# Low parts and one difference made by accumulating transfers in a decoder layer in fp32

## The chip, the cores and the metric

The kernel runs on one core of one Trainium2 chip. The metric is the device time of one launch in microseconds (us), the median of several runs. The names of the engines: PE is TensorE (matmuls), DVE is VectorE, ACT is ScalarE, POOL is GpSimd, SP is SyncE, which here only issues transfers.

## The reference

One decoder layer over 1024 tokens with model width 1024: a token mixer with two kinds of attention, then a feed-forward part (FFN) with a short convolution and a gate, width 2816, then a final norm. The change lies in the FFN and the final norm, and touches nothing of the attention.

```python
def rmsnorm(x, g):
    y = x32 * lax.rsqrt(jnp.mean(x32 * x32, axis=-1, keepdims=True) + EPS)
    return (y * g.astype(jnp.float32)).astype(x.dtype)

def conv_ffn(x, norm_g, w_up, conv_w, conv_b, w_down):
    S = x.shape[1]
    h = rmsnorm(x, norm_g) @ w_up
    hp = jnp.pad(h, ((0, 0), (CONV_W - 1, 0), (0, 0)))
    hc = conv_b
    for i in range(CONV_W):
        hc = hc + hp[:, i:i + S] * conv_w[i]
    gate, up = jnp.split(hc, 2, axis=-1)
    return (jax.nn.silu(gate) * up) @ w_down

def reference(x, attn_norm, ..., final_norm):
    h = h + token_mixer(rmsnorm(h, attn_norm[l]), ...)
    h = h + conv_ffn(h, ffn_norm[l], w_up[l], conv_w[l], conv_b[l], w_down[l])
    return rmsnorm(h, final_norm)
```

## The kernel before

**Arithmetic.** All products are to be good to fp32. A matrix is split into a high part, which is a copy rounded to the type fp32r, and a low part, which is the rest: low = x - high, rounded as well. A product is the sum of three passes (`acc3`, L1005 to L1008): high x high, high x low and low x high. ACT makes the high part with a copy, and `sub` makes the low part by a subtraction: on DVE its line is L95, on POOL L97. PE reads the low part of a weight block in the third matmul of the first three.

**Stages.** Attention takes the first 650 us, the product with w_o the next 72 (`wo_tiles`). During these the residual x is formed and its squares are summed for the FFN's norm: `cols` sums columns with ones on PE (L173), `rows` makes the reciprocal root on DVE and ACT (`rmv` L178, `rmt` L179, `rmr` L180 to L183) and spreads it over the partitions with PE (L193), and eight steps scale x by it (L1042 on DVE, high part `nh` L1047 on ACT, low part `nl` L95 on DVE).

**The FFN's up product** (722 to 1153 us) is made in 22 pairs, a gate block and an up block of 128 columns each. A pair is computed as seven products of half size, j = 0 to 6 (`Pair.run`), whose weights are a11, s2, a12, s3, s1, a22, s4: j = 0, 2 and 5 are plain halves of loaded blocks, the others are sums and differences of them. `Weights.parts` (L1138) makes the high and the low part of one of the seven. A product has 12 matmuls of 128x512. The parts are made six products ahead (AHEAD). In the first five pairs (CROWDED) all sums and all low parts are made on DVE, later ones are shared with POOL. For the first three pairs products 6 and 3 run early (`run_early`), into q, which ACT evacuates (L1172). DVE evacuates the others to hg and u (L1192), and the convolution and the gate run on ACT and DVE (L1080 to L1092).

**The FFN's down product** (from 1153 us) is made in seven products as well, in the order of the list `down`: "2", then "6" and "5" step by step in turn, then "1" and "7" in turn, "4" and "3", each of 11 steps k over 128 rows. `fetch_down` loads four steps ahead, `prep_down` makes the operands two steps ahead on DVE (L1277) and their parts on ACT (L1314) and DVE (L95). At "6" s2 = st - a11 is formed, of two k in one tile (`s`); "5" uses st; at "3" s2 becomes a12 - s2, for which a12 is loaded again (L1253). The results of products are summed into c and p tiles of two blocks of 128 columns each (L1335), and x is added by accumulating transfers issued by POOL (L1338): such a transfer reads memory and adds to what stands in the tile.

**The end.** The last three steps of "3" are held back and run in two halves of 256 tokens (`tail`, 128x256 matmuls). Each half is summed, squared, scaled by the final norm and its gains, and written out. Six of eight blocks of 128 columns are scaled by DVE straight from PSUM (L1419), two by POOL (L1460).

**Order.** Each engine runs its instructions in one fixed order, which a scheduler of the program sets when the kernel is built; `later(n, ...)` delays a step by n products. Each engine waits at an instruction until its inputs are there, and all behind it wait too. Transfers issued by SP and by POOL are queued on their engine the same way.

Of the kernel before, what the change touches and what calls it, by code (L numbers as in the profile page):

```python
# [17 lines left out]
P = 128  # L18
# [31 lines left out]
def body(ctx: ExitStack, tc: tile.TileContext, io, out):  # L50
# [1063 lines left out]
    class Weights:  # L1114
# [23 lines left out]
        def parts(self, j, new):  # L1138
            x = self.get(("a11", "s2", "a12", "s3", "s1", "a22", "s4")[j])
            t = new([P, 2, 4, P], F32R, "wp")  # L1140
            act(t[:, 0], x, AF.Copy)  # L1141
            sub("dve" if j % 2 or self.m < CROWDED else "pool", t[:, 1], x, t[:, 0])
            return t
# [101 lines left out]
    def fetch_down(i):  # L1245
# [5 lines left out]
        def get(n, ap):  # L1251
            live[n, k] = t = half([P, 512], name=n)
            load(t, ap)  # L1253

        if name in "23":
            get("a12", bottom[:, :512])
        if name in "24":
            get("b21", hid_d[KF + k][:, :512])
# [12 lines left out]
    def prep_down(i):  # L1271
# [15 lines left out]
        elif name == "6":  # L1287
            live["st", k] = st = big([P, 2, 512], name="st")
            if k % 2 == 0:
                t = big([P, 2, 512], name="s2")  # L1290
                live["s2", k], live["s2", k + 1] = t[:, 0], t[:, 1]
            a, b = live["s2", k], half([P, 512], name="t2")
            tt(dve, st[:, 0], a21, add, g["a22"])
            tt(dve, st[:, 1], b12, minus, b11)
            tt(dve, a, st[:, 0], minus, a11)
            tt(dve, b, g["b22"], minus, st[:, 1])
# [12 lines left out]
        else:  # L1309
            a, b = g["s2"], g["b22"]  # L1310
            tt(dve, a, g["a12"], minus, a)
        ops[name, k] = wide([P, 2, 512], F32R, "wp"), big([P, 2, 512], F32R, "bp")
# [55 lines left out]
    def after(name):  # L1368
# [4 lines left out]
        elif name in "65":  # L1373
            block_tiles("p" + name)
            for m in range(4):
                act(at("p" + name, m), b[m], AF.Copy)
        elif name == "1":
# [19 lines left out]
        elif name == "4":  # L1397
# [14 lines left out]
            for m in range(4):  # L1412
                later(12 + 2 * m, lambda m=m: outs[1].add(at("p5", m)))
            for m in (2, 3):
                later(20 + m, lambda m=m: act(at("p5", m), at("p5", m), AF.Copy, scale=col(C_ON + 4 + m)))

# [9 lines left out]
    def tail():  # L1426
# [9 lines left out]
        for t in range(2):  # L1436
            s = slice(t * 256, (t + 1) * 256)
            for m in (0, 2, 1, 3):
# [7 lines left out]
                if m < 3:  # L1446
                    sum_into(dve, outs[1].sq[:, s], q, outs[1].sq[:, s])
                sq[t] = q
                if t == 1 and m == 2:
                    cols(0)  # L1450
        rs[0] = rms_rows(None, rc[0])
        cols(1)
        for t in range(2):
# [4 lines left out]
            act(r, rs[t], AF.Copy)  # L1458
            y = res["p5"][1][:, :, s]
            pool.tensor_tensor(out=y, in0=y, in1=r[:, None, :].to_broadcast([P, 2, 256]), op=OP.mult)  # L1460
            for m in range(KD - 2):
                finish("c12" if m < 4 else "p5", m % 4, m, s, rs[t], 1)
            put_out(KD - 2, 1, s, y)

# [142 lines left out]
```

## Time and profile before

| | before |
|---|---|
| median of 3 runs | 1388.72 us (1386.17 to 1388.74) |
| profiled execution, its own time | 1389.71 us |
| its span in the profile | 1387.9 us |
| PE busy | 1348.8 us (97%) |
| DVE busy | 1022.8 us (74%) |
| ACT busy | 669.5 us (48%) |
| POOL busy | 412.0 us (30%) |

The span runs from the first to the last instruction of the profile. A matmul's row gives its start and its modelled length; since matmuls overlap, the distance between two starts says more than the length. In a row of the timeline what stands in brackets is the idle time ahead of the instruction and the instruction that ended it. PEclk is the granted clock of TensorE, 1.00 for its full speed of 2.4 GHz; its other level is 1.2 GHz.

### The profile page before, as it was taken

How to read it: one execution, taken by the hardware profiler on the slowest of the kernel's cores; microseconds unless marked ns; L12 is line 12 of the kernel's file. 1: busy time of each engine (PE TensorE's matmuls, PEld its weight loads, DVE VectorE, ACT ScalarE, POOL GpSimd, SP SyncE). 2: the span in 40 equal slices, each digit the busy share in tenths (PEclk: the TensorE clock that was granted, in tenths of full speed). 3: DMA queues.
4: the chain of work that ended last, by engine and by line, in shares of the span. 5: the costliest groups of instructions: out<-in, count | busy, mean ns of one | idle time of the engine just before them, and what ended most of it. 6: DMA issues, size and time to landing. Idle time of an engine off the chain costs nothing.

```text
span 1387.9 us, 18985 instructions
## 1 busy us (share of the span) xinstructions
PE 1348.8 (97%) x6996; PEld 1088.5 (78%) x6996; DVE 1022.8 (74%) x1626; ACT 669.5 (48%) x1213; POOL 412.0 (30%) x363
## 2 busy tenths in 40 slices
PE   9999999999999999999998999999999999999996
PEld 7788888767777767778887778888888888888785
DVE  5465465677766666684689997777878778998796
ACT  6032124667666555672445544444444444354362
POOL 4300524043334334210000035665666550000100
PEclk9999999999999999999999999999999999999998
DMA  5323436011121145744741222222221247743543
GB/s 212 130 96 101 157 107 199 15 46 40 50 72 49 43 125 146 210 140 147 257 145 42 80 91 92 77 75 76 91 91 71 73 146 258 277 165 138 153 140 122
DMA packets 69117, 164.58 MB, mean 119 GB/s; under 512 B 9288, under 2 KB 22744, under 8 KB 69024
## 3 DMA queue, kind: packets, MB, share of 16 engines
q1 hardware_dynamic: 56624, 132.16, 28.6%
q0 software_dynamic: 9520, 26.61, 6.4%
q10 hardware_dynamic: 2880, 4.60, 0.9%
q8 instruction: 55, 0.90, 0.3%
q14 instruction: 38, 0.31, 0.1%
HBM read 126.25 MB, written 37.09 MB: 118 GB/s over the span
## 4 chain that ended last, share of the span: by engine, by line
PE 59%; DVE 23%; ACT 7%; issue 4%; POOL 4%; DMA 1%; DVEq 0%; ACTq 0%; POOLq 0%
PE A L632 8%; PE O L669 8%; DVE wp L95 7%; PE B L654 6%; PE A L203 4%; PE A L204 4%; PE A L206 4%; PE B L1006 3%; PE B L1008 3%; PE B L1007 3%; PE A L1006 3%; PE A L1008 3%; ACT hc L1080 3%; PE A L1007 3%; DVE hg L1192 3%
## 5 line engine op out<-in xcount | busy, mean ns | idle before, releaser
L643 ACT ACTIVATE p<-p,low 128x640 f32<-128x640 f32 (+7 forms) x192 | 142.6, 744 | 48.7 <-DVE low L640 46.6
L1006 PE MATMUL B<-hi,wp 128*128 128x512 f32 x340 | 132.8, 391 | 1.0 <-DVE hg L1192 1.0
L1007 PE MATMUL B<-lo,wp 128*128 128x512 f32 x340 | 132.4, 390 | 0.0
L1008 PE MATMUL B<-hi,wp 128*128 128x512 f32 x340 | 132.2, 389 | 0.0
L654 PE MATMUL B<-ident,p 128*128 128x128 f32 x816 | 122.8, 275 | 4.4 <-ACT pt L609 1.6
L97 POOL TENSOR_TENSOR wp<-w,wp 128x512 fp32r<-128x512 f32 x34 | 56.3, 1657 | 229.3 <-ACT wp L1141 229.3
L654 PEld LDWEIGHTS B<-ident,p 128*128 128x128 f32 x816 | 96.2, 140 | 22.5 <-issue 5.8
L1141 ACT ACTIVATE wp<-ws 128x512 fp32r<-128x512 f32 x88 | 53.6, 628 | 99.9 <-DVE ws L1135 64.7
L95 DVE TENSOR_TENSOR wp<-ws,wp 128x512 fp32r<-128x512 f32 x54 | 66.9, 1243 | 44.6 <-ACT wp L1141 44.6
L203 PE MATMUL A<-hi,hi 128*128 128x512 f32 (+1 forms) x228 | 89.8, 394 | 1.5 <-DVE z L211 1.5
L609 ACT ACTIVATE pt<-B 128x512 f32<-128x512 f32 (+3 forms) x134 | 64.2, 480 | 52.0 <-PE B L654 51.4
L612 DVE COPY pt<-B 128x512 f32<-128x512 f32 (+3 forms) x154 | 77.4, 509 | 15.9 <-PE B L654 15.0
L204 PE MATMUL A<-lo,hi 128*128 128x512 f32 (+1 forms) x228 | 88.8, 390 | 0.0
L1080 ACT ACTIVATE hc<-hg,prm 128x1024 f32<-128x1024 f32 x44 | 54.5, 1243 | 66.3 <-DVE hg L1192 66.2
L103 ACT ACTIVATE hi<-w 128x1024 fp32r<-128x1024 f32 (+2 forms) x34 | 34.7, 1023 | 96.2 <-PE A L204 61.5
L1082 DVE SCALAR_TENSOR_TENSOR hc<-hg,prm,hc 128x1022 f32<-128x1022 f32 x44 | 78.1, 1775 | 0.6
L1006 PE MATMUL A<-nh,wp 128*128 128x512 f32 x188 | 74.3, 395 | 3.7 <-ACT q L1172 3.7
L669 PE MATMUL O<-pt,vsw 128*64 128x256 f32 x528 | 76.4, 387 | 0.0
L1081 DVE SCALAR_TENSOR_TENSOR hc<-hg,prm,hc 128x1023 f32<-128x1023 f32 x44 | 58.1, 1320 | 24.0 <-ACT hc L1080 23.9
L1006 PEld LDWEIGHTS B<-hi,wp 128*128 128x128 f32 x340 | 64.0, 188 | 14.9 <-issue 1.3
L1007 PEld LDWEIGHTS B<-lo,wp 128*128 128x128 f32 x340 | 64.0, 188 | 13.3 <-DVE lo L95 0.2
L1008 PEld LDWEIGHTS B<-hi,wp 128*128 128x128 f32 x340 | 63.9, 188 | 13.3
(328 smaller groups left out, 3667.1 us busy)
## 6 DMA issues: line engine op xcount, KB each, us to landing
w<-in_w_up SPq DMA_DIRECT2D x50, 512.0 KB, 3.3
hidd<-hid SPq DMA_DIRECT2D x22, 512.0 KB, 2.6
w<-in_w_down SPq DMA_DIRECT2D x22, 512.0 KB, 3.4
a<-in_w_down SPq DMA_DIRECT2D x44, 256.0 KB, 4.9
b<-hidd SPq DMA_DIRECT2D x33, 256.0 KB, 5.1
w<-in_w_o SPq DMA_DIRECT2D x16, 512.0 KB, 3.4
x<-in_xT SPq DMA_DIRECT2D x15, 512.0 KB, 6.3
rb<-scr POOLq DMA_DIRECT2D x48, 128.0 KB, 2.9
```

Source lines behind the costliest of these rows:

```text
L95: dve.tensor_tensor(out=o, in0=a, in1=f(b), op=OP.subtract)
L203: mm(outs[c], wh, hs[c], start=start, stop=False)
L204: mm(outs[c], wh, ls[c], start=False, stop=False)
L632: mm(a[:, s, :w], lh, rh[:, s * w:(s + 1) * w], start=j == 0, stop=j == len(passes) - 1)
L643: act(p, p, AF.Exp, bias=low, scale=-1.0, accum_out=r["total"])
L654: nc.tensor.transpose(b[:, k * P:(k + 1) * P], self.rows[y]["p"][:, (4 * q + k) * P:(4 * q + k + 1) * P], ident)
L669: mm(o[64 * x:64 * x + 64, z * P:2 * P], self.value(x, k), self.pt[x, k // 4][:, k % 4, z:, :], start=k == 0, stop=k == last - 1, skip_gro ...
L1006: mm(b, wh, h, start=start, stop=False, skip_group_check=skip)
L1007: mm(b, wh, l, start=False, stop=False, skip_group_check=skip)
L1008: mm(b, wl, h, start=False, stop=stop, skip_group_check=skip)
L1080: later(n, lambda: act(o, x, AF.Identity, bias=col(C_CB + m), scale=w[2]))
L1082: later(n + 6, lambda: dve.scalar_tensor_tensor(o[:, 2:], x[:, :T - 2], w[0], o[:, 2:], op0=OP.mult, op1=OP.add))
```

## The change

There are three parts.

- In the first five pairs, the low parts of j = 0, 2 and 5 (the plain weights) are no longer subtracted on DVE. ACT writes the negative of the high part into the low part's place (L1144 of the changed kernel), and a transfer issued by POOL (L1146) adds the weight block from memory to it, 256 KB each, 15 in all.
- The difference `s` of "6" is stored with the other sign, a11 - st. The product of "6" is evacuated with scale -1 for that. Transfers issued by POOL add a12 from memory (L1265, five of 512 KB and one of 256 KB), so that "3" finds a12 - s2 there. The 11 loads of a12 and the 11 subtractions at "3" are gone.
- At the end ACT multiplies c12 and p5 by the gains first (in 128x256 and 128x512 pieces, `gain`), and the last step is one multiplication per two blocks, 128x2x256: three on DVE and one on POOL for each half (L1476).

```diff
@@ -1139,7 +1139,13 @@
             x = self.get(("a11", "s2", "a12", "s3", "s1", "a22", "s4")[j])
             t = new([P, 2, 4, P], F32R, "wp")
             act(t[:, 0], x, AF.Copy)
-            sub("dve" if j % 2 or self.m < CROWDED else "pool", t[:, 1], x, t[:, 0])
+            if j in (0, 2, 5) and self.m < CROWDED:
+
+                act(t[:, 1], f(t)[:, 0], AF.Copy, scale=-1.0)
+                k = 4 if j else 0
+                side(t[:, 1], io["w_up"][self.m + (NF if j == 5 else 0)][:, k:k + 4], accum_op=OP.add)
+            else:
+                sub("dve" if j % 2 or self.m < CROWDED else "pool", t[:, 1], x, t[:, 0])
             return t
 
     def block_product(o, w, j, start, stop):
@@ -1252,8 +1258,12 @@
             live[n, k] = t = half([P, 512], name=n)
             load(t, ap)
 
-        if name in "23":
+        if name == "2":
             get("a12", bottom[:, :512])
+        if name == "4" and k % 2 == 0:
+            n = min(2, KF - k)
+            side(live["s2pair", k][:, :n], io["w_down"][(KF + k) * P:(KF + k + n) * P, :512]
+                 .rearrange("(k p) m -> p k m", k=n), accum_op=OP.add)
         if name in "24":
             get("b21", hid_d[KF + k][:, :512])
         if name in "64":
@@ -1287,12 +1297,12 @@
         elif name == "6":
             live["st", k] = st = big([P, 2, 512], name="st")
             if k % 2 == 0:
-                t = big([P, 2, 512], name="s2")
+                live["s2pair", k] = t = big([P, 2, 512], name="s2")
                 live["s2", k], live["s2", k + 1] = t[:, 0], t[:, 1]
             a, b = live["s2", k], half([P, 512], name="t2")
             tt(dve, st[:, 0], a21, add, g["a22"])
             tt(dve, st[:, 1], b12, minus, b11)
-            tt(dve, a, st[:, 0], minus, a11)
+            tt(dve, a, a11, minus, st[:, 0])
             tt(dve, b, g["b22"], minus, st[:, 1])
         elif name == "5":
             a, b = g["st"][:, 0], g["st"][:, 1]
@@ -1308,7 +1318,6 @@
             tt(dve, b, b, minus, b11)
         else:
             a, b = g["s2"], g["b22"]
-            tt(dve, a, g["a12"], minus, a)
         ops[name, k] = wide([P, 2, 512], F32R, "wp"), big([P, 2, 512], F32R, "bp")
         for x, t in ((a, ops[name, k][0]), (b, ops[name, k][1])):
             act(t[:, 0], x, AF.Copy)
@@ -1373,7 +1382,7 @@
         elif name in "65":
             block_tiles("p" + name)
             for m in range(4):
-                act(at("p" + name, m), b[m], AF.Copy)
+                act(at("p" + name, m), b[m], AF.Copy, scale=-1.0 if name == "6" else 1.0)
         elif name == "1":
             block_tiles("p1")
             for m in range(4):
@@ -1411,8 +1420,12 @@
             outs[1] = Out()
             for m in range(4):
                 later(12 + 2 * m, lambda m=m: outs[1].add(at("p5", m)))
-            for m in (2, 3):
-                later(20 + m, lambda m=m: act(at("p5", m), at("p5", m), AF.Copy, scale=col(C_ON + 4 + m)))
+            for m in range(4):
+                later(20 + m, lambda m=m: gain("p5", m, 4 + m, slice(0, 512)))
+
+    def gain(name, j, m, s):
+        x = at(name, j)[:, s]
+        act(x, x, AF.Copy, scale=col(C_ON + m))
 
     def finish(name, j, m, s, rs, c):
         x = at(name, j)[:, s]
@@ -1446,6 +1459,7 @@
                 if m < 3:
                     sum_into(dve, outs[1].sq[:, s], q, outs[1].sq[:, s])
                 sq[t] = q
+                gain("c12", m, m, s)
                 if t == 1 and m == 2:
                     cols(0)
         rs[0] = rms_rows(None, rc[0])
@@ -1456,11 +1470,11 @@
                 rs[1] = rms_rows(None, rc[1])
             r = half([P, 256], name="rst")
             act(r, rs[t], AF.Copy)
-            y = res["p5"][1][:, :, s]
-            pool.tensor_tensor(out=y, in0=y, in1=r[:, None, :].to_broadcast([P, 2, 256]), op=OP.mult)
-            for m in range(KD - 2):
-                finish("c12" if m < 4 else "p5", m % 4, m, s, rs[t], 1)
-            put_out(KD - 2, 1, s, y)
+            for e, by, name, j in ((pool, r, "p5", 1), (dve, rs[t], "c12", 0), (dve, rs[t], "c12", 1),
+                                   (dve, rs[t], "p5", 0)):
+                y = res[name][j][:, :, s]
+                e.tensor_tensor(out=y, in0=y, in1=by[:, None, :].to_broadcast([P, 2, 256]), op=OP.mult)
+                put_out(2 * j + (4 if name == "p5" else 0), 1, s, y)
 
     h1.fetch(0)
     wo_prep(0)
```

The instructions move in three places that matter for what follows. On DVE, ahead of the first norm of the FFN, the rows are these before (wp: weight parts; ws: sums of weights; rmv to rmr: the norm's row chain; rs: its spread copy):

```order
L1135 TENSOR_TENSOR ws_7091<-ws_7089,w_7082 128x512
L95 TENSOR_TENSOR wp_7099<-ws_7089,wp_7099 128x512
L95 TENSOR_TENSOR wp_7109<-w_7105,wp_7109 128x512
L95 TENSOR_TENSOR wp_7093<-ws_7091,wp_7093 128x512
L95 TENSOR_TENSOR wp_7102<-w_7083,wp_7102 128x512
L178 TENSOR_SCALAR rmv_7131<-B_7126 128x4
L180 RECIPROCAL rmr_7133<-rmt_7132 128x4
L181 SCALAR_TENSOR_TENSOR rmt_7132<-rmr_7133 128x4
L182 TENSOR_TENSOR rmt_7132<-rmt_7132,rmv_7131 128x4
L183 SCALAR_TENSOR_TENSOR rmr_7133<-rmt_7132,rmr_7133 128x4
L197 COPY rs_7152<-B_7153 128x512
```

and these after:

```order
L1135 TENSOR_TENSOR ws_7092<-ws_7090,w_7082 128x512
L95 TENSOR_TENSOR wp_7101<-ws_7090,wp_7101 128x512
L178 TENSOR_SCALAR rmv_7135<-B_7130 128x4
L95 TENSOR_TENSOR wp_7094<-ws_7092,wp_7094 128x512
L180 RECIPROCAL rmr_7137<-rmt_7136 128x4
L181 SCALAR_TENSOR_TENSOR rmt_7136<-rmr_7137 128x4
L182 TENSOR_TENSOR rmt_7136<-rmt_7136,rmv_7135 128x4
L183 SCALAR_TENSOR_TENSOR rmr_7137<-rmt_7136,rmr_7137 128x4
L197 COPY rs_7156<-B_7157 128x512
```

Two low parts that stood directly ahead of `rmv` are gone (two more a little further up are gone too), and one more low part now stands behind it.

On PE, at the turn from pair 3 to pair 4, the rows are these before (A and B: PSUM banks; nh, nl, hi, lo: parts of the tokens):

```order
L1006 MATMUL B_7696<-hi_7278,wp_7558 128x512
L1007 MATMUL B_7696<-lo_7279,wp_7558 128x512
L1008 MATMUL B_7696<-hi_7278,wp_7558 128x512
L1006 MATMUL A_7749<-nh_7166,wp_7627 128x512
L1007 MATMUL A_7749<-nl_7167,wp_7627 128x512
L1008 MATMUL A_7749<-nh_7166,wp_7627 128x512
L1006 MATMUL A_7749<-nh_7166,wp_7627 128x512
L1007 MATMUL A_7749<-nl_7167,wp_7627 128x512
```

and these after, from the last three of pair 3's a22 on:

```order
L1006 MATMUL B_7643<-hi_7317,wp_7593 128x512
L1007 MATMUL B_7643<-lo_7318,wp_7593 128x512
L1008 MATMUL B_7643<-hi_7317,wp_7593 128x512
L1006 MATMUL A_7764<-nh_7170,wp_7639 128x512
L1007 MATMUL A_7764<-nl_7171,wp_7639 128x512
L1008 MATMUL A_7764<-nh_7170,wp_7639 128x512
L1006 MATMUL B_7710<-nh_6810,wp_7614 128x512
L1007 MATMUL B_7710<-nl_6811,wp_7614 128x512
```

Before, pair 4's a11 (wp_7627) runs ahead of pair 3's a22 (wp_7582); after, pair 4's a11 (wp_7639) comes behind it (wp_7593), 12 matmuls later, and is left after three matmuls for other work.

On POOL, behind its last product of the gate, the rows of the changed kernel are these (s: the stored differences of "6"; c and p: results to which x is added):

```order
L1092 TENSOR_TENSOR hid_10289<-hc_10205,hc_10206 128x1024
L1092 TENSOR_TENSOR hid_10449<-hc_10337,hc_10338 128x1024
L1265 DMA s_10573<-in_w_down 128x2x512
L1265 DMA s_10663<-in_w_down 128x2x512
L1265 DMA s_10765<-in_w_down 128x2x512
L1265 DMA s_10865<-in_w_down 128x2x512
L1265 DMA s_10965<-in_w_down 128x2x512
L1265 DMA s_11058<-in_w_down 128x512
L1347 DMA c_11617<-x2d 128x2x512
L1347 DMA c_11618<-x2d 128x2x512
L1347 DMA p_11170<-x2d 128x2x512
```

Before, the transfers into c follow the rows of L1092 directly. The six new ones stand between them, and each waits only for the subtractions that fill its tile.

## Rows read from the trace of the kernel before

**Rows 1.** Waits of PE in 700 to 860 us: total, times, longest.

```profile
PE A L1006 <- ACT q L1172: 3.7, 1, 3.7
PE B L1006 <- DVE hg L1192: 3.6, 2, 2.6
```

**Rows 2.** Waits of PE in 1325 to 1388 us.

```profile
PE A L1006 <- ACT wp L1314: 1.9, 1, 1.9
```

**Rows 3.** Stretches: length, then busy us of each engine, PEclk, DMA share, GB/s.

```profile
800.00:820.00 20.00, 18.54 (x81) 14.74 (x79) 19.83 (x21) 9.65 (x14) 9.57 (x5) 1.00 0.28 97
820.00:840.00 20.00, 18.82 (x76) 15.43 (x77) 14.80 (x16) 7.97 (x11) 8.42 (x5) 0.91 0.23 88
```

**Rows 4.** Timeline of PE, 736 to 744 us: start, length, engine, line, operation.

```profile
737.83 0.79 PE L1006 MATMUL A<-nh,wp 128*128 128x512 f32 x1 [3.67 <-ACT q L1172]
...
743.54 0.41 PE L1007 MATMUL B<-lo,wp 128*128 128x512 f32 x1
```

**Rows 5.** Timeline of PE, 765 to 797 us.

```profile
765.65 0.39 PE L1008 MATMUL B<-hi,wp 128*128 128x512 f32 x1
...
796.58 0.39 PE L1007 MATMUL A<-nl,wp 128*128 128x512 f32 x1
796.81 0.39 PE L1008 MATMUL A<-nh,wp 128*128 128x512 f32 x1
```

**Rows 6.** Line L1277: duration min/median/max in ns, first and last start.

```profile
L1277 DVE TENSOR_TENSOR s<-a,s x11: 676/681/683, 1332.2 to 1362.4; 128x512 f32<-128x512 f32 x11
```

**Rows 7.** Chain that ended last, 715 to 830 us: start, length, what.

```profile
787.92 0.60 DVE wp L95
```

**Rows 8.** Timeline of PE, 1361 to 1367 us.

```profile
1361.59 0.28 PE L1007 MATMUL A<-bp,wp 128*128 128x256 f32 x1
1361.70 0.28 PE L1008 MATMUL A<-bp,wp 128*128 128x256 f32 x1
...
1366.52 0.41 PE L1007 MATMUL A<-bp,wp 128*128 128x256 f32 x1
1366.73 0.41 PE L1008 MATMUL A<-bp,wp 128*128 128x256 f32 x1
```

**Rows 9.** Timeline of DVE, 722 us.

```profile
722.20 0.15 DVE L178 TENSOR_SCALAR rmv<-B 128x4 f32<-128x4 f32 x1
```

**Rows 10.** Timeline of DVE, first and last of eleven low parts of plain weights.

```profile
746.54 0.69 DVE L95 TENSOR_TENSOR wp<-w,wp 128x512 fp32r<-128x512 f32 x1
...
803.37 0.68 DVE L95 TENSOR_TENSOR wp<-w,wp 128x512 fp32r<-128x512 f32 x1
```

**Rows 11.** Timeline of ACT, 753 to 792 us, two high copies.

```profile
753.70 0.62 ACT L1141 ACTIVATE wp<-w 128x512 fp32r<-128x512 f32 x1
...
791.30 0.62 ACT L1141 ACTIVATE wp<-w 128x512 fp32r<-128x512 f32 x1
```

**Rows 12.** Line L1338, the four accumulating transfers of 512 KB.

```profile
DMA to landing us min/median/max: 7.3/8.6/11.2
```

**Rows 13.** Transfers in 1300 to 1325 us by queue: packets, MB, share of 16 engines.

```profile
q0 software_dynamic: 1067, 2.09, 49.0%
q1 hardware_dynamic: 2004, 3.71, 46.9%
```

**Rows 14.** Transfers in 1180 to 1240 us, queue, and issues with median us to landing.

```profile
q1 hardware_dynamic: 5034, 14.11, 66.0%
...
b<-hidd SPq DMA_DIRECT2D x7, 512.0 KB, 4.6
```

**Rows 15.** Timeline of SP, 1183 to 1196 us.

```profile
1189.10 0.38 SPq L1265 DMA_DIRECT2D b<-hidd  x1
```

**Rows 16.** Timeline of DVE, 1198 us.

```profile
1198.42 0.69 DVE L1277 TENSOR_TENSOR st<-b 128x512 f32<-128x512 f32 x1
```

**Rows 17.** Chain that ended last, whole run.

```profile
1317.45 6.88 DMA a<-in_w_down
```

**Rows 18.** Timeline of DVE, 1378 us.

```profile
1378.22 0.47 DVE L1419 SCALAR_TENSOR_TENSOR c<-c,prm,B 128x256 f32<-128x256 f32 x1
```

## The prediction

> **What bounds the kernel now.** The waits of TensorE (PE) come first, since PE is the engine with almost no idle time. Between 700 and 860 us it waits three times: 3.7 us for ScalarE's (ACT) copy q, and twice, 3.6 us together, for VectorE's (DVE) evacuation hg [rows 1]. At the end one wait stands out, 1.9 us for a high part of the last product's weights [rows 2]. Then the table of stretches, for who is late: in 800 to 820 us DVE is busy 19.83 us of 20 and PE 18.54, and in 820 to 840 PE's clock is 0.91 [rows 3]. So in these places DVE, not PE, sets the pace, and work taken off DVE there can become time. Where PE doesn't wait (pairs 5 to 21, most of the down products) the change can only cost.
>
> A stall costs more than itself. After the wait that ends at 737.83 the next 13 matmuls take 5.71 us until 743.54 [rows 4]; at their usual 0.23 us apart [rows 5] they would take 2.96, so 2.75 us go to the lower of PE's two clock levels. After the longer of the two waits for hg, 2.6 us up to about 821, comes the 0.91 [rows 3]: 9% of 20 us is 1.8, and I take 1.6 since the second decimal is rounded. The other, of 1.0 us [rows 1], has no such loss behind it.
>
> **Removed: 11 subtractions in the last product.** Each `s` subtraction (L1277) takes 0.68 us in its row [rows 6], and DVE starts its next instruction 0.60 us behind it, as it does behind a low part [rows 7]: 11 x 0.60 = 6.6 us. They all start in 1332 to 1362 us, ahead of the last weight block, which PE waits for. PE stands from 1361.70 to 1366.52 where 8 matmuls of 256 columns, 0.12 us each, belong [rows 8]: 4.82 - 0.96 = 3.86 us lost. DVE running 6.6 us ahead covers that; I leave 0.3 for the last two small waits, which are for sums of PE's own output: **-3.6**. Behind it 23 matmuls run 0.21 us apart [rows 8] and not 0.12: without the stall these 2.1 us come back: **-2.1**. What is late next is the final norm (below).
>
> **Removed: 15 low parts in pairs 0 to 4.** Each is 0.60 us of DVE. Four stand ahead of the row sums of the first norm (`rmv`, 722.20 [rows 9]); the order shows `rmv` moved ahead and PE's broadcast L193 eight matmuls earlier, 8 x 0.23 = 1.8 us. The norm's steps run from that L193 through DVE and ACT to q, and the wait for it ends at 737.83 [rows 4], and PE's work ahead of the wait is the same amount; the wait of 3.67 us becomes 1.85. DVE can be there: 4 x 0.60 = 2.4 us less work puts `rmv` near 720, its chain needs 2 us, and L193 will want it at 723.1. Whether a wait of 1.85 us still lowers the clock I can't read: 1.0 did not, 2.6 did, and the 1.9 of [rows 2] did. I take a fall as short as the one of 821 (1.6 and not 2.75). Together 1.8 + 1.1 = **-2.9**; ends -1.8 (same fall) and -4.6 (none).
>
> From 751 to 820 the chain of what ended last is nearly all DVE. Eleven more of the subtractions stand between 746.54 and 803.37 [rows 10], seven of them before PE's shorter wait near 787: 4.2 us, plus the 1.8 by which the norm's chain is earlier, makes DVE 6.0 earlier where PE is 2.9 earlier. This is 3.1 ahead against a wait of 1.0: gone, 2.1 left. The other four make it 4.5 against 2.6: gone as well, and with it the lowered clock: 3.6 + 1.6 = **-5.2**. If a third of the lead is lost again the second wait still goes.
>
> **Added on ACT.** 15 negative copies, each about a high copy's 0.62 us [rows 11], within some 100 us in which ACT is about half busy, and 8 small gains ahead of the last matmuls' end, where ACT mostly waits. Mostly behind a high copy and ahead of nothing that waits: 0, at worst 0.6 us at one norm step, inside the range.
>
> **Added: accumulating transfers for the 15 low parts.** The trace has none of 256 KB. The four of 512 KB (L1338) land 7.3 to 11.2 us after issue [rows 12]; half the bytes should be near half of that, 3.7 to 5.6, and 11.2 is the other bound. What covers it is the time from the high part's copy to PE's first use of the low part. At the tightest of the blocks that keep their place, pair 1's a22, this is 753.70 + 0.62 to 765.65 [rows 5, 11], 11.3 us; less 0.6 for the negative copy it holds even a slow landing. The exception is pair 4's a11, 791.30 + 0.62 to 796.81 [rows 5, 11], 4.9 us. The new order runs pair 3's last 12 matmuls first (+2.7), and DVE's lead over PE grows by 2.1, giving 9.7; its negative copy now stands behind a conv step (L1080) that waits for DVE, and costs some 2. So 7.7 us against a likely 5.6: 0; with 11.2 it costs 3.5 us plus 1.6 of clock. Both stay in the range. The issues stand on POOL's queue, idle here; its next work, pair 5's first low part, is queued behind the fifteenth issue. That block's high copy is also later on ACT, so nothing new is waited for.
>
> The Trainium skill has a rule that speaks against giving transfers to this queue ("SBUF — State Buffer", Who interferes with whom): a DMA that looks stalled by a DVE instruction is one issued by GpSimd, starved of descriptor-port time; it adds that tensor_tensor takes the read side only. DVE's work in these stretches is almost all of that kind, and the four transfers at hand landed within 11.2 us beside a DVE that was busy all the time; no run here shows the plainer copies beside one. By the rule at its worst each issue would wait for a gap in DVE, which is the second rival's price.
>
> **Added: six accumulating transfers into `s` (L1265), and 11 loads gone from 1320 to 1347.** They are written at "4" but POOL has nothing else to do and they wait for DVE's subtractions alone, so they start at about 1183, 1196, 1207, 1218, 1229 and 1235 us, among the heaviest loads of the program. Price: in 1300 to 1325, 2.09 MB of accumulating traffic took 49.0% of the 16 engines' time and 3.71 MB of loads 46.9% [rows 13], 2.1 times as much per byte, or 3.1 us of all engines per 512 KB: 25 x 0.49 / 4. Six with 2.88 MB take 17 us. Loads took 66.0% of 1180 to 1240 [rows 14], 39.6 us; 56.6 of 60 in all. A 512 KB load of `b` issued at 1189.10 [rows 15] is first read by DVE at 1198.42 [rows 16], 9.3 us later, and such loads land in 4.6 [rows 14]: some 4.7 us of lead. One transfer delays the loads beside it by about 3.1 (a 256 KB load beside two of them took 6.88 us [rows 17]). I take **+1.0** for a spot where two delays meet, ends 0 and +3.
>
> The rule behind that is in the Trainium skill ("DMA: Bandwidth & Descriptors", Issuing engines are not separate DMA queues): transfers of all issuing engines end on the same 16 engines and interleave. The trace agrees by the 6.88 us just named. A second queue therefore buys no bandwidth, and the sum has +1.0 for it where separate queues would give 0.
>
> **The end.** The first half's final multiplications are mixed with the second half's row chain: four of 0.39 us apart (0.47 in the row [rows 18]) become three of twice the size, by low parts of 512 elements 0.60: 1.8 against 1.6. After it, 3 x 0.60 stand against 6 x 0.40, but the last out waits in order behind POOL's. **+0.2**, ends -0.5 and +0.6.
>
> **Sum**: -3.6 - 2.1 - 2.9 - 5.2 + 1.0 + 0.2 = -12.6. The profiled execution took 1389.7, giving 1377.1; it lies 1.0 above the median of the runs, 1388.7, from which the sum gives 1376.1. I say **1376**.
>
> **Rivals.** (1) The wait at 734 gets short enough to leave the clock up, and transfers collide with nothing: -4.6 for -2.9 and 0 for +1.0, 1373.4. For it: 1.85 lies between waits with and without a fall. (2) Transfers land late at a few blocks (pair 4's a11, pair 1's a22): 3.5 + 1.6 once and 1 to 2 elsewhere give back 5 to 7, 1381 to 1383. For it: tight leads and a price taken from four rows; against it: half the bytes. (3) Slower: the six transfers of L1265 hold up the loads of "6" and "5" for as long as they are under way, and not for their share. With the shortest landing in the trace, 7.3 us [rows 12] for 512 KB, 2.88 MB hold the loads for 40 us. 20.4 of the 60 us are free and 4.7 are lead: 15 us are lost, in about three waits that lower the clock at 1.6 each. That is +19.9 in place of +1.0: -12.6 - 1.0 + 19.9 = +6.3, or 1395. It ends slower by over 0.2% from 6.7 us of hold each, with the 16 engines then busy without a gap over 1185 to 1240. Against it: the 6.88 us of a load beside two transfers is less than one such hold. (4) The change doesn't do what it says: the stalls of PE are not DVE's backlog but a PSUM bank or a load; then 1388 to 1389. Against it: the waits name DVE, or ACT behind it.
>
> **How the numbers follow.** The forecast 0.53 (its own range 1373.5 to 1380), rival 1 0.18, rival 2 0.16, rival 3 0.08, rival 4 0.05. Range 1371 to 1385: rivals 3 and 4 lie above it, 0.13, and a few of 100 below. A change within 0.2% (2.8 us) is what a measurement of this kernel can't tell from none. Faster 0.87, same 0.05, slower 0.08.
>
> **What would show it.** Right: no waits of PE on hg L1192 at 786 and 818; a wait near 734 of about 1.9 us; no wait on ACT wp L1314 at the last held steps and no lowered clock before the last matmul; DVE below 20 of 20 in 760 to 820 and 1340 to 1360; PE's waits in 1185 to 1240 below 2 us. Wrong: PE waiting on POOL's queue for a low part in pairs 1 to 4 (rival 2), or the DMA share at 1.0 and DVE waiting for `b` loads in 1185 to 1240 (rival 3).

## The result and the profile after

The changed kernel takes 1377.43 us (median of 4 runs, 1376.06 to 1378.34), the kernel before 1387.45 on the same chip (4 runs, 1385.69 to 1388.74): a ratio of 0.9931, 95% interval 0.9917 to 0.9945. It is faster by 0.7%, 7.6 to 11.5 us. The forecast was 1376, and the time lies 1.4 us above it; the gain of 12.6 us that it was made of lies above the 7.6 to 11.5.

The profiled execution took 1377.45 us with a span of 1375.7, against 1389.71 and 1387.9: 12.3 and 12.2 us less. That is more than the medians show, 10.0: the before's profiled execution is among its slowest, 2.3 us above the median, and the terms of the forecast were read from it. To see where the 12.2 come from, I took the same matmul in both traces and compared its start. "Gained" below is the shift since the line before.

| stretch, by the after's time | forecast | gained | what the after shows there |
|---|---|---|---|
| 730 to 755, wait for q | -2.9 | -2.5 | wait 1.86 for 3.67, a shorter lowered clock |
| 755 to 874, pairs 0 to 5 | -5.2 | -3.6 | two waits for hg gone, one new |
| 874 to 1349, other pairs and most of the down product | +1.0 | -0.1 | no wait, b loads slower |
| 1349 to the last matmul | -5.7 | -6.7 | stall on the weights gone, and one for L193 |
| behind the last matmul | +0.2 | +0.5 | fewer, wider multiplications |
| sum | -12.6 | -12.4 | |

(The after's trace lies 0.2 us later than the before's at 730 us, hence -12.2 in the span.)

The waits of PE in 680 to 860 us, total, times and longest, answer to [rows 1]:

```profile
PE A L1006 <- ACT q L1178: 1.9, 1, 1.9
PE B L1008 <- DVE lo L95: 1.4, 1, 1.4
PE B L1006 <- DVE hg L1198: 1.0, 1, 1.0
```

The wait for q is half as long. The middle one, near 693, is outside the stretch of [rows 1] and unchanged. The last one is new: it is for hg as the two of [rows 1] were, but in another place. Here are all three of its links, first PE's wait, then DVE's step ahead of it, then SP's queue (start, length, what, and in brackets the idle time ahead and what ended it):

```profile
797.75 0.50 PE L1006 MATMUL B<-nh,wp 128*128 128x512 f32 x1 [1.01 <-DVE hg L1198]
```
```profile
788.69 0.69 DVE L1135 TENSOR_TENSOR ws<-w 128x512 f32<-128x512 f32 x1 [1.60 <-DMA w<-in_w_up]
```
```profile
768.53 13.92 SPq L1093 DMA_DIRECT2D hidd<-hid  x2
782.54 0.38 SPq L1123 DMA_DIRECT2D w<-in_w_up  x1
```

Read from the bottom: SP issued one store of `hid` at 768.53 and stood until 782.12 at the next (the row merges the two), whose data weren't made yet. The load of pair 4's up weights, queued behind it, went out at 782.54 and landed 6.1 us later, at 788.66. DVE stood 1.6 us for it, and PE 1.0 for DVE. In the kernel before the same load was issued at 788.55 behind the same kind of store and landed in 3.4 us, 0.7 us before DVE wanted it.

The timeline of PE at the wait for q answers to [rows 4]:

```profile
736.20 0.50 PE L1006 MATMUL A<-nh,wp 128*128 128x512 f32 x1 [1.86 <-ACT q L1178]
...
737.24 0.55 PE L1007 MATMUL A<-nl,wp 128*128 128x512 f32 x1
737.59 0.63 PE L1008 MATMUL A<-nh,wp 128*128 128x512 f32 x1
...
740.58 0.47 PE L1006 MATMUL B<-hi,wp 128*128 128x512 f32 x1
```

Behind the wait the first matmuls still run 0.23 us apart; from 737.24 to 740.58 eight take 3.34 us instead of 1.84 and the modelled length is 0.63 instead of 0.39, the lower of the two clock levels. This costs 1.5 us where 2.75 were lost before. The stretches (length, busy us of PE, PE's loads, DVE, ACT and POOL, PEclk, DMA share, GB/s) answer to [rows 3]:

```profile
720.00:740.00 20.00, 18.14 (x79) 14.72 (x80) 16.96 (x28) 10.38 (x16) 1.67 (x2) 0.93 0.31 79
...
800.00:820.00 20.00, 20.00 (x89) 16.16 (x88) 15.83 (x17) 9.14 (x14) 8.30 (x5) 1.00 0.38 121
820.00:840.00 20.00, 20.00 (x89) 16.40 (x88) 15.88 (x17) 8.67 (x13) 10.34 (x7) 1.00 0.23 83
...
1340.00:1360.00 20.00, 20.00 (x118) 17.57 (x118) 14.92 (x31) 8.66 (x19) 0.00 (x0) 1.00 0.27 106
```

In 800 to 820 DVE went from 19.83 busy to 15.83 and PE from 18.54 to 20.00; in 820 to 840 the clock went from 0.91 to 1.00. In 1340 to 1360 PE has no gap. There the eight matmuls that took 4.82 us in [rows 8], counted from the first matmul of the program, take 1.25:

```profile
1354.77 0.39 PE L1007 MATMUL A<-bp,wp 128*128 128x256 f32 x1
...
1356.02 0.28 PE L1007 MATMUL A<-bp,wp 128*128 128x256 f32 x1
```

The fifteen new transfers (line L1146: duration of the issue in ns, first and last start, then issue to landing) and the traffic in 1180 to 1240 us (packets, MB, share of the 16 engines; loads with KB and us to landing), which answers to [rows 14]:

```profile
L1146 POOL DMA_DIRECT2D wp<-in_w_up x15: 851/860/1083, 712.5 to 797.5; - x15
...
DMA to landing us min/median/max: 3.9/5.1/7.2
```
```profile
q1 hardware_dynamic: 4498, 12.90, 60.7%
q0 software_dynamic: 1490, 2.86, 27.9%
...
b<-hidd SPq DMA_DIRECT2D x7, 512.0 KB, 6.4
```

### The profile page after: what moved, and what is told of

It reads as the page before. It is cut to its first block, busy times and chain, and to the rows that moved or that the text cites. A ratio compares the mean times of both kernels' runs of the same rounds, so it can differ in the third digit from the quotient of the medians.

```text
span 1375.7 us, 19011 instructions
## 1 busy us (share of the span) xinstructions
PE 1343.7 (98%) x6996; PEld 1083.3 (79%) x6996; DVE 1005.2 (73%) x1594; ACT 682.7 (50%) x1238; POOL 430.3 (31%) x384
## 4 chain that ended last, share of the span: by engine, by line
PE 63%; DVE 17%; ACT 7%; issue 5%; POOL 4%; DMA 1%; DVEq 0%; ACTq 0%; SPq 0%; POOLq 0%
PE A L632 8%; PE O L669 8%; PE B L654 6%; DVE wp L95 5%; PE B L1008 5%; PE B L1006 5%; PE B L1007 4%; PE A L203 4%; PE A L204 4%; PE A L206 4%; PE A L1006 4%; PE A L1008 4%; PE A L1007 4%; ACT hc L1080 3%; DVE hg L1198 2%
## 5 line engine op out<-in xcount | busy, mean ns | idle before, releaser
L95 DVE TENSOR_TENSOR wp<-ws,wp 128x512 fp32r<-128x512 f32 x54 | 65.2, 1211 | 46.9 <-ACT wp L1141 46.8
L1141 ACT ACTIVATE wp<-ws 128x512 fp32r<-128x512 f32 x88 | 53.6, 629 | 87.6 <-DVE ws L1135 57.5
L1007 PE MATMUL A<-nl,wp 128*128 128x512 f32 x188 | 73.9, 393 | 0.0
```

What stands on the lines that cost most here:

```text
L95: dve.tensor_tensor(out=o, in0=a, in1=f(b), op=OP.subtract)
L1007: mm(b, wh, l, start=False, stop=False, skip_group_check=skip)
```

## The experiments

Each short diff is against the changed kernel, except for the first three, which are parts of the change put alone into the kernel before. Executions of the same code differ by up to 3 us in where the work behind 268 us starts, and by 1.7 us more in 400 to 500, so shifts between traces are counted from the same matmul at about 700 us.

**The three parts by themselves.** First the fifteen low parts:

```
+            if j in (0, 2, 5) and self.m < CROWDED:
+                act(t[:, 1], f(t)[:, 0], AF.Copy, scale=-1.0)
+                ...
+                side(t[:, 1], io["w_up"][...], accum_op=OP.add)
```

> Only the first part of the change: the 15 low parts by accumulating transfers, all else as before. Theory (DVE's backlog sets PE's waits in pairs 0 to 4, and the stretch gives its gain independently of the end): 5.5 to 6.5 us faster than before, with the wait for q near 734 at 1.9 us, no wait of 2.6 us near 818, and the whole end (1.9 us wait for ACT wp L1314, lowered clock) as before. Rival (the gain at the end needs the earlier one, or the pairs' gain is lost again later): under 4 us.

Measured: 1382.30 us, 0.9957 (0.9943 to 0.9971). The last matmul starts 6.8 us earlier, 6.3 of these by 1335. PE's waits in 680 to 860 and at the end:

```profile
PE A L1006 <- ACT q L1178: 1.9, 1, 1.9
...
PE B L1006 <- DVE hg L1198: 1.1, 1, 1.1
```
```profile
PE B L193 <- DVE rmr L183: 2.3, 2, 2.2
PE A L1006 <- ACT wp L1320: 1.9, 1, 1.9
```

The new wait for hg comes with this part, and the stall at the weights stays. Then the difference in the last product:

```
+        if name == "4" and k % 2 == 0:
+            side(live["s2pair", k][:, :n], io["w_down"][...], accum_op=OP.add)
...
-            tt(dve, a, g["a12"], minus, a)
```

> Only the second part: the 11 subtractions and 11 loads at product 3 replaced by six accumulating transfers and the changed sign, all else as before. Theory: 6 to 7 us faster than before, all of it after 1345 us: no wait for ACT wp L1314 and full clock up to the last matmul; the pairs as before. Rival (the new form of the last multiplications and gains has a share in it): 4 to 5 us here, and 1 to 2 in the run with the third part alone.

Measured: 1381.85 us, 0.9956 (0.9943 to 0.9969). The pairs gain 0.45 us, and 6.7 come after 1345: 0.9 at L193 and 5.8 at the weights. The waits in 680 to 860 are those of [rows 1], with one of 0.5 us for a high part (ACT wp L1141) beside them, and at the end none for a high part is left:

```profile
PE A L1006 <- ACT q L1172: 3.7, 1, 3.7
...
PE B L1006 <- DVE hg L1192: 3.6, 2, 2.7
```
```profile
PE B L193 <- DVE rmr L183: 2.2, 1, 2.2
PE B L1007 <- DVE bp L95: 0.6, 2, 0.4
```

Last the gains on ACT and the wider multiplications at the end:

```
-            for m in (2, 3):
+            for m in range(4):
+                later(20 + m, lambda m=m: gain("p5", m, 4 + m, slice(0, 512)))
...
```

> Only the third part: gains on ACT and the last multiplications by pairs of blocks, all else as before. Theory (from the profile after, where the end behind the last matmul is 0.3 to 0.5 us longer): 0.3 us slower, between -0.3 and +0.8. Rival: 1 to 2 us faster.

Measured: 1387.84 us, 0.9999 (0.9989 to 1.0008, 12 runs). It is worth nothing that can be timed. In the trace it is 0.8 slower behind the last matmul, and that matmul starts 2.3 us earlier; that this is no gain of the part is shown below, under the tail. The product of the three ratios is 0.9912, the change has 0.9931: the parts add up, within the intervals.

**Do the transfers cost anything?** The six of L1265 with a sixteenth of their bytes (so most of a12 is left out of the differences), and then twice over:

```
-            side(live["s2pair", k][:, :n], io["w_down"][..., :512]
+            side(live["s2pair", k][:, :n, :32], io["w_down"][..., :32]
```

> The changed kernel with the six transfers of L1265 cut to 32 of 512 columns each (a sixteenth of the bytes; a12 is then missing from most of s). Every engine's order is that of the changed kernel, so only the traffic of 2.7 MB is gone. Theory (the loads' lead covers the traffic): same time as the changed kernel within 0.7 us, with loads of b landing in about 4.6 us again and not 6.4. Rival (the traffic costs time that the two profiles hide): 1 us faster or more.

Measured: 1376.17 us, 0.9913 (0.9899 to 0.9926). By the medians this is 1.3 us faster than the changed kernel, but the trace is 1.8 us ahead of the changed kernel's already at 268 us and all the way on; within 1150 to 1245 the shift is 0.0. Their share fell from 27.9% to

```profile
q0 software_dynamic: 1232, 0.15, 4.4%
```

and the b loads land in 4.8 us for 6.4. So the six cost the loads 1.6 us of landing and PE nothing.

```
+            side(live["s2pair", k][:, :n], io["w_down"][(KF + k) * P:(KF + k + n) * P, :512]
+                 .rearrange("(k p) m -> p k m", k=n), accum_op=OP.add)
```

> The changed kernel with each of the six transfers of L1265 made twice, one behind the other (a12 is then added twice). An accumulating transfer is then under way for most of 1178 to 1240. By share (0.279 of 60 us for six, and loads 0.607) the engines would need 1.17 of the stretch. Theory A (a transfer costs the loads its share, 3 us per 512 KB, and the loads lead by 4.7 us): the stage is past its edge, some of the second transfers slip behind 1240, DVE and PE lose 0 to 4 us in 1185 to 1245. Rival 3 of the prediction (loads stand while a transfer is under way): the loads stop nearly altogether, 15 us or more slower.

Measured: 1379.52 us, 0.9947 (0.9934 to 0.996). The trace is 1.9 us behind, all of it between 1185 and 1243. PE's waits from 1150 on (two of the three for bp, 0.6 us, stand at the end, as in the changed kernel) and the traffic in 1180 to 1240:

```profile
PE B L1007 <- DVE bp L95: 1.1, 3, 0.5
PE B L1006 <- ACT bp L1325: 0.4, 1, 0.4
```
```profile
q1 hardware_dynamic: 4371, 12.27, 55.1%
q0 software_dynamic: 2428, 4.69, 43.8%
...
b<-hidd SPq DMA_DIRECT2D x7, 512.0 KB, 9.4
```

With 98.9% of the engines' time taken the loads land in 9.4 us, a little more than the 9.3 that the first b load had until its use [rows 15, 16], and only then does PE wait: 0.9 us in the rows, and 1.9 by the trace's shift. The rival in which each transfer holds the loads as long as it is under way asked for 15 us or more: it is out. What decides is the share of the engines that is left for the loads. The Trainium skill ("DMA: Bandwidth & Descriptors", Issuing engines are not separate DMA queues) says that transfers of all issuing engines run on the same 16 DMA engines and interleave. The trace agrees: the loads went on beside the transfers, at 55.1% beside 43.8%.

**Where did the pairs lose 1.6 us of their 5.2?** Two remedies for the new wait. One gives the fifteen transfers a quarter of their bytes (the weight is left out of the rest of these low parts), the other takes the `hid` stores of the first five pairs off SP's queue:

```
-                side(t[:, 1], io["w_up"][...][:, k:k + 4], accum_op=OP.add)
+                side(t[:, 1, :, :32], io["w_up"][...][:, k:k + 4, :32], accum_op=OP.add)
```

> The changed kernel with the 15 transfers of L1146 cut to 32 of 128 columns of each block (a quarter of the bytes; the low parts are then mostly minus the high part). Every engine's order is that of the changed kernel. In the changed kernel's profile DVE idles 1.6 us at 787 for a load of pair 4's weights, and PE then waits 1.0 us at 796. Theory A (that load was issued late, behind a store on SP's queue, and the traffic matters little): the wait of about 1.0 us for hg stays, the time is that of the changed kernel within 0.6 us. Theory B (the load of 6.1 us was slowed by the accumulating traffic beside it): the load lands in 3 to 4 us, both waits go, 1.2 us faster.

```
-            move(hid_d[m], h)
+            (side if m < CROWDED else move)(hid_d[m], h)
```

> The changed kernel with the stores of hid of the first five pairs (L1093) issued by POOL and not by SP; the orders on PE, DVE and ACT are unchanged. SP's queue then doesn't stand at a store that waits for DVE, and the load of pair 4's weights behind it can go out as soon as its buffer is free. Theory A of the run before: DVE's wait of 1.6 us at 787 and PE's of 1.0 us at 796 are gone, 1.0 to 1.4 us faster than the changed kernel. Theory B: the load still takes 6 us but starts earlier, so the wait goes as well; if the wait stays, the load was held by its buffer, and neither is right.

Measured: 1375.49 us, 0.9917 (0.9905 to 0.993), and 1375.99, 0.9923 (0.9911 to 0.9935). In both the wait at 797 is gone and the shift there is -1.4 us. With small transfers the load of pair 4's up weights leaves where it did, seen from PE's work near 694 us, behind the same store; it lands in 4.5 us and not in 6.1, just in time, and DVE's step, with no idle time ahead of it, starts 1.65 us earlier. With the stores on POOL the load leaves 1.8 us earlier (that trace lies 0.6 us ahead at 694) and lands in 3.3 us:

```profile
780.08 0.33 SPq L1123 DMA_DIRECT2D w<-in_w_up  x1
```

So the late issue alone doesn't make the wait: it needs the slow landing, which the transfers' bytes make. That the slow landing alone would not make it is not shown, since the second remedy took both away; sent off at 780.08 and 6.1 us under way, the load would have come 0.2 us behind DVE's step at 785.99.

**Is the wait for q one of order or of DVE's work?** The last four norm steps four ticks later, so that ACT makes q earlier:

```
-        later(9 + m, lambda m=m: h0.norm(m))
+        later((9 if m < 4 else 13) + m, lambda m=m: h0.norm(m))
```

> The changed kernel with the last four norm steps of the first half handed over four products later, so that ACT's copy q stands behind three high parts nh and not behind all eight, and the first sum of tokens (L1104) stands ahead of the last two norm steps on DVE. Theory A (the wait of 1.9 us at 734 is ACT's order alone): the wait goes, and with it the lowered clock: 3 us faster than the changed kernel. Theory B (DVE's work on the norm and the sums of tokens is what ends last in 722 to 742): the wait for q goes, PE waits at 737 to 739 for low parts lo instead, 0 to 1.2 us faster.

Measured: 1377.16 us, 0.9927 (0.9915 to 0.9939). The wait for q is gone, and an equal one stands 18 matmuls later, for the high part of a sum of tokens that DVE makes from the norm's outputs (L1104). In the pairs the wait for hg at 797 is gone, and two for u, 2.5 us in all, are new. In the trace, counted from 700 us, this run is 1.2 us behind the changed kernel's, which the medians don't show:

```profile
738.68 0.50 PE L1006 MATMUL B<-hi,wp 128*128 128x512 f32 x1 [1.90 <-ACT hi L103]
739.76 0.63 PE L1007 MATMUL A<-nl,wp 128*128 128x512 f32 x1
```
```profile
PE B L1006 <- DVE u L1198: 2.5, 2, 1.3
```

The 0.63 of the second row is the lowered clock again. ACT's order is not what bounds here; DVE's norm steps and sums of tokens are.

**Do the last five low parts pay?** Pair halves a22 made by DVE again:

```
-            if j in (0, 2, 5) and self.m < CROWDED:
+            if j in (0, 2) and self.m < CROWDED:
```

> The changed kernel with the low parts of a22 (j = 5) of the first five pairs made on DVE again, so 10 of the 15 by transfers. The order puts PE's broadcast L193 three matmuls later than in the changed kernel. Theory (each low part is 0.6 us of a DVE that is behind): the wait at 734 grows from 1.9 to 2.5 us; in the pairs 4 x 0.6 = 2.4 us of DVE's lead are lost, so waits for hg of about 0.5 us near 787 and 1 to 1.5 us near 800 to 818 come up; 2 to 3 us slower than the changed kernel, with no clock fall after 800. Rival (the lead is large enough for ten, the last five low parts bought nothing): under 0.8 us slower.

Measured: 1376.42 us, 0.9927 (0.9914 to 0.9939), no slower than the change; I had expected 2 to 3 us. PE's waits in 680 to 860:

```profile
PE A L1006 <- ACT q L1178: 2.5, 1, 2.5
...
PE B L1006 <- DVE u L1198: 0.7, 1, 0.7
PE B L1006 <- DVE hg L1198: 0.3, 1, 0.3
```

These five gain 0.7 us at q and 1.6 at 815 to 836, and they bring the 1.0-us wait at 797 with 0.3 behind it and 0.4 in small gaps ahead of it. In the trace this leaves 0.6 us for them.

**Can the six subtractions ahead of the norm be had on POOL?** With the stores on POOL and six low parts of pairs 0 to 2 made there too:

```
+                sub("dve" if (j % 2 or self.m < CROWDED) and (j != 6 and j != 3 or self.m > 2) else "pool", ...)
```

> The changed kernel with the stores on POOL, and the six low parts of sums that the first three pairs make early (675 to 716 us) on POOL and not on DVE. DVE is busy 20.0 of 20 us in 680 to 700, and PE waits 1.4 us at 693 for a low part of w_o. Theory A (DVE's backlog): 3.6 us of DVE go, the wait at 693 goes, 1.4 us faster than with the stores alone. Theory B (POOL's subtractions slow DVE's by sharing, as near 810 us, where steps of 1.2 us take 2.2): the wait stays or grows, 0 to 1 us slower.

Measured: 1377.26 us, 0.9928 (0.9915 to 0.9942), 1.3 us behind the same kernel without them by the medians, which is within the intervals; in the traces, counted from 700 us, it is 2.3. A wait of 1.3 us for a square (L173) is new, and the expected gain is not there. The wait near 693 stays as it was, but this run can't tell what makes it: in the changed kernel DVE makes the six low parts between 703 and 715 us, behind that wait.

**All pairs.** With the stores on POOL, transfers make the three low parts in all 22 pairs, and then, from pair 5 on, a22's alone:

```
+            if j in (0, 2, 5):
```

> The changed kernel with the stores of hid as in the run before last (POOL) and the low parts of a11, a12 and a22 by transfers in all 22 pairs, not in five. In the later pairs PE loses 0.25 us per pair, 15 times, to a late evacuation hg of a DVE that is slowed beside POOL's subtractions. Theory A (POOL's tensor work slows DVE, and taking two of its subtractions and one of DVE's per pair away ends it): the 0.25 us per pair go, 3 to 4 us faster than the run with the stores alone. Theory B (the 0.25 us are the evacuation's own place in the order, no engine is behind there): no change, within 0.7 us. If the transfers land late: slower.

```
+            if j in (0, 2, 5) and (j == 5 or self.m < CROWDED):
```

> As the run with transfers in all 22 pairs, but from pair 5 on only the low part of a22 (j = 5, DVE's own subtraction) comes by a transfer; those of a11 and a12 stay subtractions on POOL. Theory A (DVE's own subtraction, which stands between two evacuations hg, makes PE late): all of the gain stays, 4 to 5.5 us faster than with the stores alone (ratio to before near 0.989). Theory B (POOL's subtractions slow DVE beside them, and their going was the gain): most of the 0.25 us per pair stays, 0 to 1.5 us faster than with the stores alone (ratio near 0.992).

Measured: 1371.61 us, 0.9888 (0.9874 to 0.9901), and 1373.31, 0.9886 (0.9869 to 0.9902). The two can't be told apart by time, and both are faster than the change and than the kernel before. In pairs 5 to 21 the first is 5.5 us ahead of the changed kernel's trace and the second 3.3; in the first the clock also stayed up behind the wait for q, worth 1.0, though its work up to there is the changed kernel's. (The first has two new waits before that, 0.6 us for a low part of the tokens at 743 and 0.7 for hg at 816.) The stretch 900 to 1000 us, of the changed kernel, of the second and of the first:

```profile
900.00:1000.00 100.00, 99.62 (x434) 80.82 (x433) 79.41 (x73) 43.55 (x63) 60.25 (x36) 1.00 0.23 79
```
```profile
900.00:1000.00 100.00, 99.99 (x440) 81.75 (x439) 77.32 (x69) 47.32 (x66) 64.88 (x42) 1.00 0.29 93
```
```profile
900.00:1000.00 100.00, 100.00 (x443) 82.83 (x442) 73.44 (x69) 54.89 (x79) 54.31 (x43) 1.00 0.49 121
```

PE seemed full here, which is why I had said that the change can only cost in these pairs. But 99.6% hid 0.2 to 0.3 us at an evacuation in each of 15 pairs, too short for the table of waits. One of them in the changed kernel, 0.50 us between two starts where 0.23 is usual:

```profile
893.39 0.39 PE L1008 MATMUL B<-hi,wp 128*128 128x512 f32 x1
893.89 0.50 PE L1006 MATMUL B<-nh,wp 128*128 128x512 f32 x1
```

DVE, of the changed kernel, of the second of the two and of the first:

```profile
893.16 0.68 DVE L1198 TENSOR_TENSOR hg<-B,u 128x512 f32<-128x512 f32 x1
893.76 1.16 DVE L95 TENSOR_TENSOR wp<-w,wp 128x512 fp32r<-128x512 f32 x1
894.85 0.68 DVE L1198 TENSOR_TENSOR hg<-B,p 128x512 f32<-128x512 f32 x1
```
```profile
892.89 0.69 DVE L1198 TENSOR_TENSOR hg<-B,p 128x512 f32<-128x512 f32 x1 [0.27 <-PE B L1008]
```
```profile
891.18 0.68 DVE L1198 TENSOR_TENSOR hg<-B,u 128x512 f32<-128x512 f32 x1
892.56 0.69 DVE L1198 TENSOR_TENSOR hg<-B,p 128x512 f32<-128x512 f32 x1 [0.70 <-PE B L1008]
```

In the changed kernel the subtraction for a22 stands between two evacuations on which PE's next bank depends; without it DVE is there ahead and waits for PE, by 0.27 us with a22 alone and by 0.70 with all three. So a22 gives 3.3 of the 5.5 us, less than all of it and more than little, which were the two forecasts. The other 2.2 go with a11 and a12, whose subtractions POOL made; by the traces DVE's own then run faster (the one ahead of these rows takes 0.69 us and not 1.01), but no run tests that by itself.

## Why the prediction was right, and where it was not

**The bound.** The waits named DVE, and taking work from DVE gave the time: [rows 1, 3] were read rightly for pairs 0 to 4, and the stall of [rows 2, 8] was DVE's backlog. The second rival is out by the trace after, in which PE waits for none of the fifteen low parts, the third (held loads) by the runs with small and doubled transfers, the fourth by the result.

**The tail, -5.7, measured -5.8 and 0.9 more.** The 6.6 us that DVE got covered the stall of 3.86, and the lowered clock behind it went as well. What I didn't count is 0.9 us at the broadcast L193 near 1350, where PE waited 0.65 before. That wait goes back to a load. ACT waited for a block `a` of w_down, DVE 2.08 us for ACT, and the row chain of the norm, behind it on DVE, came late. The waits of ACT in the kernel before and in the run with the gains alone, whose work is the same up to there:

```profile
1324.42 0.63 ACT L1314 ACTIVATE wp<-a 128x512 fp32r<-128x512 f32 x1 [2.12 <-DMA a<-in_w_down]
```
```profile
1322.11 0.63 ACT L1314 ACTIVATE wp<-a 128x512 fp32r<-128x512 f32 x1 [1.12 <-DMA a<-in_w_down]
```

The load took 6.88 us in the kernel before, 6.37 with the low parts alone and 5.90 with the gains alone, and the wait at L193 was 0.65, 0.15 and none. So in these runs it changes with the execution and is no gain of the change; how much of the 0.9 is the change's own stays open. The lowered clock changes as well: behind the same stall 24 matmuls ran 0.21 us apart in the kernel before and 13 with the gains alone, which is 1.0 us. The run with the second part alone took 11 loads away together with the 11 subtractions, and no run separates the two; the trace before, with DVE busy for all of 1340 to 1360, speaks for the subtractions.

**The wait for q, -2.9, measured -2.5.** The wait became 1.86 where I had worked out 1.85. The clock fell behind it, as I had guessed from the 1.9 of [rows 2], for a stretch that cost 1.5 where I had taken 1.6. The few tenths that are missing are lost in small gaps up to 745. The first rival needed the clock to stay up, and here it did not.

**The pairs, -5.2, measured -3.6: the term that failed.** The step on DVE's lead held: both waits and the lowered clock at 821 are gone. The sentence on the leftover lead ("If a third of the lead is lost again the second wait still goes") came true as it stands; what failed is the step behind it, that nothing else is lost there. A DVE that is 3 us earlier also wants its inputs 3 us earlier, and I asked that only of the low parts. The load of pair 4's up weights stood behind a store in SP's queue, and the fifteen transfers beside it stretched its landing from 3.4 to 6.1 us (4.5 with a quarter of their bytes). The prediction had counted a share of the DMA engines for the six large transfers and none for these fifteen, though they crowd into 85 us. The price is the 1.0 us of the wait and 0.3 behind it; the experiments that remove it gain 1.4, most of the 1.6 that are missing.

**The low parts' landing.** Forecast 3.7 to 5.6 us, measured 3.9 to 7.2. The tight block, pair 4's a11, was issued at 788.04 and first read at 796.35 without a wait.

**The six transfers, +1.0, measured -0.1.** The engine time was right, 17 us forecast and 27.9% of 60 = 16.7 measured. (The prediction's 2.1 times per byte is misread: 49.0% for 2.09 MB against 46.9% for 3.71 MB is 1.9. Its 3.1 us per transfer doesn't rest on that.) The b loads went from 4.6 to 6.4 us, and the lead of 4.7 swallowed this; I had allowed for two delays that meet, and they don't. Doubled, the same transfers cost 1.9.

**The end, +0.2, measured +0.5.** In nine other traces with the new end it is 0.8 to 1.2, in a tenth 2.0, so the upper end of +0.6 was too low.

So between the two traces the sum is right to 0.2 us because errors of -1.0 (tail), -1.1 (transfers), +0.4 and +1.6 (q, pairs) nearly cancel, with 0.3 at the end. That is luck, and so is the time: it was counted from a median of 1388.7, which with a fourth run is 1387.45, and from there the same sum gives 1374.9, 2.6 us below the measured time. By the medians the gain is 10.0 us. The late load and the longer lowered clock in the trace before, 0.9 and 1.0 us, would make up most of the difference to 12.4; that is an estimate. Only the runs by parts show that the mechanisms were the ones named.

**Still open.** Whether the clock falls behind a wait of 1.9 us can't be read from the wait. Eight traces have one of 1.86 us for q. In seven the clock fell behind it (in 720 to 740 us it is 0.93 in the changed kernel). In the version with transfers in all pairs, whose work up to there is the same, it stayed at 1.00, worth 1.0 us.

## What to carry to other kernels

An engine that is made earlier wants all its inputs earlier: after work has been taken off it, follow each of its other inputs, too, and look at what stands ahead of their loads in the queue, a store that waits for its data above all. Price an added transfer by the share of the DMA engines that it takes in the busiest stretch, and set the slower landing of the neighbours against the lead that they have. And a full engine in a table of busy shares can still lose 0.3 us each time round a loop: compare the starts of the same instruction over many rounds before you call a stage unable to gain.

## What the runs showed of the hardware

An accumulating transfer takes about twice the engine time of a plain one per byte: 27.9% for 2.86 MB against 60.7% for 12.90 MB is 2.1 times, and [rows 13] gives 1.9. Up to 89% of the engines' time it cost PE nothing, at 99% 1.9 us.

A subtraction on DVE with both inputs in SBUF takes 0.69 us by itself and 1.0 to 2.2 beside tensor work of POOL, while the evacuations, with one input from PSUM, keep 0.68 through all the pairs. These are such a subtraction of the changed kernel, the operation on POOL beside it, and the 44 evacuations of one kind:

```profile
887.61 2.21 DVE L95 TENSOR_TENSOR wp<-ws,wp 128x512 fp32r<-128x512 f32 x1 [2.06 <-ACT wp L1141]
```
```profile
886.87 2.40 POOL L1092 TENSOR_TENSOR hid<-hc,hc 128x1024 f32<-128x1024 f32 x1
```
```profile
L1198 DVE TENSOR_TENSOR hg<-B,u x44: 675/682/692, 754.1 to 1150.1; 128x512 f32<-128x512 f32 x44
```

The Trainium skill ("SBUF — State Buffer", Who interferes with whom) says that with two SBUF inputs DVE contends with a GpSimd instruction that reads SBUF, and with at most one it does not. The trace agrees, by the 2.21 and the 0.68 us above. The Trainium skill's warning in the same section, that a transfer which DVE seems to stall is one issued by GpSimd, did not come true beside this DVE work: the issues of L1146 took 0.85 to 1.08 us.
